# The last two expert pairs and the final LayerNorm of a transformer layer reordered across TensorE, VectorE, ScalarE and GpSimd

## Chip, cores and metric

The kernel runs on one core of one Trainium2 chip. The metric is the device time of one execution in microseconds (us); the time of the kernel before is the median of three runs.

## What is computed

One layer of a streaming encoder over 512 tokens of 1024 channels, in fp32. Only the second half of it matters here: a hierarchical mixture of experts (a group is chosen, then two experts in it), a residual, and a LayerNorm.

```python
x = _layer_norm(ALPHA * x + mixed, ln1_g, ln1_b)
ffn = _hierarchical_moe(x.reshape(b * s, d), ...)
return _layer_norm(ALPHA * x + ffn, ln2_g, ln2_b)

# one expert of 4 groups x 8, D_EXPERT = 256
hid = silu(x @ w_gate[g, e]) * (x @ w_up[g, e])
y = y + combine[:, g, e] * (hid @ w_down[g, e])
```

## The kernel before

Both attentions, the gates and the output projection fill most of the time before 418 us, where the experts begin. TensorE then runs through the 32 experts in the loop at L1332 to L1365. Each expert e has 64 slots for tokens; two experts make a pair p = e // 2, so that the gathered rows of a pair (xg, fetched by index from DRAM) are one tile of 128 x 1024. An expert's weights are six tiles of 512 KB in fp32, streamed in a fixed sequence on SP's queue (`raw_load`, L1052) and taken in the same sequence (`weights`).

The steps of an expert are these. `prep_x(p)` transposes a pair's rows on TensorE (L1108) and copies them out of PSUM, one half on ScalarE (L1086), one on VectorE (L1088). `gate_up(e)` multiplies them with four weight tiles: 16 matmuls into the PSUM tile sc, in two halves of the partitions, which ScalarE (L1134) and VectorE (L1135) add up to gus. `act(e)` transposes gus on TensorE (stp, L1142) and makes the hidden rows sg: silu on ScalarE (L1144), the product on VectorE (L1148). `down(e)` is 8 matmuls into the PSUM tile tr; ScalarE and VectorE weight the result, add the residual (L1196, L1198, L1200), and GpSimd scatters a pair's rows to the DRAM buffer y2D (`store`). The down product stands one expert late in the loop.

The last two pairs (NLATE = 2: experts 28 to 31) are called late. Their results do not go through DRAM: `down` makes their sums on VectorE (L1181), rounds them to the high part on ScalarE (L1186), and takes the low part on VectorE (L1188), both into the tile late. It needs the other half of the partitions too, for which `late_x(p)` copies xg to xo on ScalarE (L1159, L1160). A one-hot matrix stl then brings each row to its token: `fin_add` multiplies it with late into PSUM banks called fin (fin<-late,stl), two banks for each of the four token tiles of 128. The other experts' rows come back from y2D as two tiles yy per token tile (L1233, behind the last weights on SP's queue); they are added to each other on GpSimd (L1272, Y_POOL) and go into the same banks by an identity matmul (`fin_rows`, fin<-yy,ident).

`finish` works off the list FIN, which is written by hand: a word is a step, its number the expert, the tile or bank.tile. "add2.3" adds late experts to bank 2 until three are in it, "rows0" adds tile 0's row pair, "stat0.1" and "stat1.1" are the statistics of tile 1's two banks on VectorE (L1294, L1296), "root0" to "root3" the steps of the reciprocal root (`rstd_parts`: aggregation on VectorE L778, Ln and Exp on ScalarE L782 and L783, a Newton step of three operations on VectorE L786, L788, L790), "gain" the product with the LayerNorm gain on VectorE (L1312), "end" the scale by the root and the bias: for tile 3 on VectorE (L1320), for the others on ScalarE (L1328) and GpSimd (L1329). FIN_AT says behind which gate_up the first four banks are opened; late results that exist by then are added there.

TensorE's instructions run in program order wherever `in_order` is set (`pin`, `keep_in_program_order`), and so do those of the other engines that are pinned. What is not pinned is placed by a scheduler, which also sets the order of the gain rows (`gain_rows`: copies bc on VectorE, matmuls pj<-ident,bc, copies gb on ScalarE) among the work of experts 28 and 29.

Of the kernel before, what the change touches and what calls it, by code (L numbers as in the profile page):

```python
# [18 lines left out]
P = 128  # L19
# [60 lines left out]
NLATE = 2  # L80
Y_PE = ()
Y_POOL = (0, 1, 2, 3)
F_DVE = (3,)
G_ACT = ()
FIN_TAG = ("pj", "pj", "tr", "sc", "sc", "av", "tr", "tr")
FIN_AT = {30: (0, 1, 2, 3)}
FIN = (
# [16 lines left out]
def trunk(ctx, tc, xT, x, wm, wv, wbr, wout, wr, br, bg, rbx, lnp, lncol, wexp, out):  # L104
# [669 lines left out]
    def rstd_parts(pool, bs, bufs=2, between=None, eps=(epsc, EPS)):  # L774
# [16 lines left out]
        yield r, mean  # L791

    def rstd(*a, **b):
        *_, out = rstd_parts(*a, **b)
        return out
# [326 lines left out]
    def gate_up(e):  # L1122
        ps = pb.tile([P, 512], F32, tag="sc", name="sc", bufs=2)
        for c in range(C):
            if c % 2 == 0:
                w = weights()
            if e < 4:
                st = xe[0, c // 4][:, c % 4, e * CAP : (e + 1) * CAP]
            else:
                st = xp[e // 2][:, c, e % 2 * CAP : (e % 2 + 1) * CAP]  # L1130
            side = slice(c % 2 * CAP, c % 2 * CAP + CAP)
            mm(ps[side], st, w[:, c % 2 * 512 : c % 2 * 512 + 512], c < 2, c >= C - 2)
        gus[e] = bp.tile([CAP, 512], F32, tag="gus", name="gus", bufs=GUSB)
        nc.scalar.activation(gus[e], ps[CAP:], AF.Copy)  # L1134
        nc.vector.tensor_add(gus[e], gus[e], ps[:CAP])  # L1135

    hid = {}

    def act(e):
        st = pb.tile([P, 4, CAP], F32, tag="av", name="stp", bufs=1)  # L1140
        for q in range(4):
            pin(nc.tensor.transpose(st[:, q, :], gus[e][:, q * P : (q + 1) * P], ident[:CAP, :CAP]))  # L1142
        sg = bp.tile([P, 2, CAP], F32, tag="sg", name="sg", bufs=3)
        nc.scalar.activation(sg, st[:, 0:2, :], AF.Silu)  # L1144
        if e == NE - 1:
            load = nc.scalar.preload_act_table_set("natural_log_exp_and_others")
            tc.keep_in_program_order(load)
        nc.vector.tensor_mul(sg, sg, st[:, 2:4, :])  # L1148
        hid[e] = sg
# [5 lines left out]
    def late_x(p):  # L1155

        xo[p] = slot([P, D], F32, f"xo{p}", slots2)
        a, b = slice(0, CAP), slice(CAP, P)
        nc.scalar.activation(xo[p][b, S:], xg[p][a, S:], AF.Copy)  # L1159
        nc.scalar.activation(xo[p][a, :S], xg[p][b, :S], AF.Copy)  # L1160

    def down(e):
        p, odd = e // 2, e % 2
        is_late = p >= NPAIR - NLATE
        if is_late:
            late.append(hip.tile([P, D], F32R, tag="hi", name=f"late{e}"))
# [8 lines left out]
        if is_late:  # L1175
# [11 lines left out]
            for half, here in enumerate(sides):  # L1187
                pin(nc.vector.tensor_sub(  # L1188
                    late[-1][sides[1 - half], cs[half]], sums[here, cs[half]], late[-1][here, cs[half]].bitcast(F32)
# [84 lines left out]
    def finish():  # L1274

        for step in FIN:
# [20 lines left out]
            elif what == "root0":  # L1297
                parts[tt] = rstd_parts(bp, fs[tt], TT, None, (epsf, 4.0 * EPS / ALPHA**2))
                fr[tt] = next(parts[tt])
# [33 lines left out]
    for e in range(NE):  # L1333
# [16 lines left out]
        if e % 2 and 3 <= e < NE - 1:  # L1350
            prep_x(e // 2 + 1)
        act(e)
        in_order[0] = False
        if e == 4:
# [6 lines left out]
        if e == NE - 4:  # L1361
            gain_rows()
            last_rows()
        if e % 2 == 0 and e >= NE - 2 * NLATE:
            late_x(e // 2)  # L1365
    in_order[0] = True
# [117 lines left out]
```

## Time and profile before

| | |
|---|---|
| runs | 689.62, 691.15, 689.78 us |
| median | 689.78 us |
| profiled execution | 692.57 us, its span 690.8 us |
| busy: TensorE (PE) | 643.6 us, 93% of the span |
| busy: VectorE (DVE) | 417.3 us, 60% |
| busy: ScalarE (ACT) | 319.0 us, 46% |
| busy: GpSimd (POOL) | 108.2 us, 16% |
| mean granted clock of TensorE | 0.98 of full speed |

The profile is of one execution, and its rows add up to that execution's span. A timeline row is a group of equal instructions that follow each other on one engine: its start, its length, and, in brackets, how long the engine had been idle and what ended that. PEclk is the granted clock of TensorE as a share of 2.4 GHz. A share of busy time is a mean over stages with different limits, so the stages are read one by one.

### The profile page before, as it was taken

Reading aid. Unit: us, or ns where it says so; the run is one execution under the profiler, and the core shown is the slowest. Engines: PE = TensorE matmul, PEld = TensorE weight load, DVE = VectorE, ACT = ScalarE, POOL = GpSimd, SP = SyncE. Lnnn points to the kernel's source line nnn. Section 1 sums busy time; section 2 is a strip of 40 time slices with the busy share of each in tenths; the row PEclk is TensorE's granted clock in tenths of the full one; section 3 lists DMA queues with packets and bytes.
Section 4 is the critical chain, followed back from the end, with each engine's and each line's share of the span. In section 5 each row is a group of like instructions: output and inputs, shape, how many; then the busy total and the mean of one; then the engine's idle time right before and its main releaser. Section 6 shows DMA issues by size and latency. Waiting matters only on the chain.

```text
span 690.8 us, 8912 instructions
## 1 busy us (share of the span) xinstructions
PE 643.6 (93%) x3108; PEld 420.8 (61%) x3108; DVE 417.3 (60%) x850; ACT 319.0 (46%) x626; POOL 108.2 (16%) x152
## 2 busy tenths in 40 slices
PE   8999999999999999989999987999999988899782
PEld 4888788887878888878888774333434322234241
DVE  5675868678867886563935994234444333334487
ACT  5676877866755565545513223322333222223422
POOL 2012112102010110050000341112112111110233
PEclk9999999999999999999999999999999999999887
DMA  8600069202130322128774579999999999999803
GB/s 331 248 0 1 1 225 353 63 0 93 46 106 17 123 77 92 46 88 304 263 315 163 202 274 412 405 411 410 409 409 405 408 406 407 402 400 405 338 3 124
DMA packets 48032, 158.62 MB, mean 230 GB/s; under 512 B 7529, under 2 KB 7673, under 8 KB 47984
## 3 DMA queue, kind: packets, MB, share of 16 engines
q1 hardware_dynamic: 43632, 150.16, 57.2%
q0 software_dynamic: 4352, 7.85, 3.0%
q8 instruction: 26, 0.43, 0.3%
q14 instruction: 22, 0.18, 0.1%
HBM read 150.16 MB, written 15.73 MB: 240 GB/s over the span
## 4 chain that ended last, share of the span: by engine, by line
PE 60%; DVE 15%; DMA 14%; ACT 6%; issue 3%; POOL 0%; SPq 0%; DVEq 0%; POOLq 0%; ACTq 0%
PE pj L130 18%; PE sc L130 13%; DMA we<-in_wexp_dram 13%; PE pb L130 6%; PE tr L130 6%; PE po L130 4%; PE pv L130 2%; PE av L130 2%; DVE t L482 2%; DVE wl L115 2%; PE tr L536 2%; DMA raw<-in_wm_dram 1%; PE stp L1142 1%; PE pj L1108 1%; ACT wh L112 1%
## 5 line engine op out<-in xcount | busy, mean ns | idle before, releaser
L130 PE MATMUL sc<-we,xp 128*64 128x512 f32 x448 | 109.8, 613 | 7.5 <-DMA we<-in_wexp_dram 6.1
L130 PE MATMUL pj<-xh,wh 128*128 128x512 f32 x256 | 103.7, 405 | 1.1 <-ACT wh L112 1.0
L130 PE MATMUL pj<-xl,wh 128*128 128x512 f32 x256 | 100.8, 394 | 0.0
L130 PE MATMUL pj<-xh,wl 128*128 128x512 f32 x256 | 100.6, 393 | 0.0
L115 DVE TENSOR_TENSOR wl<-raw,wh 128x1024 fp32r<-128x1024 f32 (+1 forms) x57 | 69.9, 1230 | 23.1 <-ACT wh L112 22.9
L1135 DVE TENSOR_TENSOR gus<-gus,sc 64x512 f32<-64x512 f32 x32 | 21.7, 679 | 94.3 <-ACT gus L1134 94.3
L130 PE MATMUL tr<-we,sg 128*64 128x512 f32 x256 | 66.0, 626 | 3.2 <-DMA we<-in_wexp_dram 2.5
L112 ACT ACTIVATE wh<-raw 128x1024 fp32r<-128x1024 f32 (+1 forms) x57 | 58.7, 1037 | 19.0 <-DMA raw<-in_wbr_dram 4.8
L130 PEld LDWEIGHTS sc<-we,xp 128*64 128x64 f32 x448 | 27.9, 138 | 64.5 <-issue 33.2
L1134 ACT ACTIVATE gus<-sc 64x512 f32<-64x512 f32 x32 | 19.0, 594 | 101.6 <-PE sc L130 101.6
L130 PEld LDWEIGHTS pj<-xh,wh 128*128 128x128 f32 x256 | 48.4, 189 | 10.9 <-ACT wh L112 1.9
L130 PEld LDWEIGHTS pj<-xh,wl 128*128 128x128 f32 x256 | 48.3, 189 | 10.8 <-DVE wl L115 0.2
L130 PEld LDWEIGHTS pj<-xl,wh 128*128 128x128 f32 x256 | 48.5, 190 | 8.2
L130 PEld LDWEIGHTS tr<-we,sg 128*64 128x64 f32 x256 | 17.3, 141 | 44.0 <-issue 34.0
L130 PE MATMUL pb<-y,wh 128*128 128x512 f32 x128 | 40.1, 394 | 0.3 <-DVE k L345 0.3
L115 DVE TENSOR_TENSOR wl<-tr,wh 128x512 fp32r<-128x512 f32 (+1 forms) x64 | 30.9, 484 | 11.9 <-ACT wh L112 11.6
L1207 POOL DMA_INDIRECT y2D<-oe,rowi x14 | 14.0, 1000 | 145.3 <-DVE oe L1198 144.7
L489 POOL TENSOR_SCALAR_AFFINE_SELECT w<-w 128x128 f32<-128x128 f32 x32 | 16.1, 515 | 126.0 <-ACT w L486 115.2
L112 ACT ACTIVATE wh<-tr 128x512 fp32r<-128x512 f32 (+1 forms) x64 | 27.3, 428 | 12.5 <-PE tr L536 12.2
L130 PE MATMUL sc<-k,q 128*128 128x512 f32 (+3 forms) x128 | 28.5, 323 | 0.2
L536 PE MATMUL tr<-ident,w 128*128 128x128 f32 x160 | 27.8, 272 | 0.0
L1200 DVE SCALAR_TENSOR_TENSOR oe<-tr,wslot,xg 64x512 f32<-64x512 f32 x24 | 18.0, 750 | 16.3 <-PE tr L130 15.8
(227 smaller groups left out, 1218.5 us busy)
## 6 DMA issues: line engine op xcount, KB each, us to landing
we<-in_wexp_dram SPq DMA_DIRECT2D x192, 512.0 KB
raw<-in_wm_dram SPq DMA_DIRECT2D x32, 512.0 KB
raw<-in_wv_dram SPq DMA_DIRECT2D x8, 512.0 KB
y2D<-zero SPq DMA_DIRECT2D x16, 256.0 KB
raw<-in_wbr_dram SPq DMA_DIRECT2D x8, 512.0 KB
raw<-in_wout_dram SPq DMA_DIRECT2D x8, 512.0 KB
yy<-y2D SPq DMA_DIRECT2D x8, 512.0 KB
strip<-in_rbx_dram SPq DMA_DIRECT2D x8, 256.0 KB
```

Of the source, the lines that this page charges most:

```text
L112: act = nc.scalar.activation(hi, src, AF.Copy)
L115: pin((eng or nc.vector).tensor_sub(lo, src, hi.bitcast(F32)), fix == "both")
L130: pin(nc.tensor.matmul(ps, a, b, start=start, stop=stop))
L482: nc.vector.tensor_tensor_scan(out=t[:, ::-1], data0=t[:, ::-1], data1=mk[:, ::-1], initial=0.0, op0=OP.add, op1=OP.mult)
L489: nc.gpsimd.affine_select(out=blk, in_=blk, pattern=[[-1, P]], compare_op=OP.is_gt, fill=0.0, base=0, channel_multiplier=1)
L536: nc.tensor.transpose(tr[:, i * P : (i + 1) * P], w[:, off + j * P : off + (j + 1) * P], ident)
L1108: pin(nc.tensor.transpose(ps[:, c, :], xg[p][:, o : o + P], ident))
L1134: nc.scalar.activation(gus[e], ps[CAP:], AF.Copy)
L1135: nc.vector.tensor_add(gus[e], gus[e], ps[:CAP])
L1142: pin(nc.tensor.transpose(st[:, q, :], gus[e][:, q * P : (q + 1) * P], ident[:CAP, :CAP]))
L1200: nc.vector.scalar_tensor_tensor(out=dst, in0=ps[here], scalar=wslot[here, p : p + 1], in1=xg[p][here, cs], op0=OP.mult, op1=OP.add)
L1207: nc.gpsimd.indirect_dma_start(out=y2D[:, :], out_offset=bass.IndirectOffsetOnAxis(ap=rowi[:, p : p + 1], axis=0), in_=oe[p], in_offset=No ...
```

## The change

The order of the last steps is written anew. The first four fin banks are opened behind gate_up(31) instead of gate_up(30). down(31) follows down(30) at once, and the adds of experts 29, 30 and 31 come behind both. The row pairs of tiles 0 and 1 are no longer added on GpSimd: each of their two yy tiles goes through its own identity matmuls. Of the low parts of the last pair (experts 30 and 31), the second half moves from VectorE to GpSimd. The final LayerNorm's Newton step is computed by four small ScalarE operations (`rstd_act`). The operations that make gus, sg and xo are pinned to program order, and late_x stands behind an odd expert's act.

```diff
--- before.py
+++ after.py
@@ -78,15 +78,15 @@
 WHB = 3
 DEPTH = 2
 NLATE = 2
-Y_PE = ()
-Y_POOL = (0, 1, 2, 3)
+Y_PE = (0, 1)
+Y_POOL = (2, 3)
 F_DVE = (3,)
 G_ACT = ()
 FIN_TAG = ("pj", "pj", "tr", "sc", "sc", "av", "tr", "tr")
-FIN_AT = {30: (0, 1, 2, 3)}
+FIN_AT = {31: (0, 1, 2, 3)}
 FIN = (
-    "sum0 sum1 sum2 sum3 down30 add0.2 add1.2 add2.2 add3.2 down31 add0.3 add1.3 add2.3 add3.3 rows0 add0.4 add1.4 stat0.0 "
-    "stat1.0 rows1 add2.4 add3.4 root0.0 gain0.0 root1.0 gain1.0 root2.0 root3.0 end.0 open4 add4.4 open5 add5.4 rows2 "
+    "down30 down31 add0.2 add1.2 add2.2 add3.2 rows0 sum2 sum3 add0.3 add1.3 add0.4 add1.4 stat0.0 "
+    "stat1.0 add2.3 add3.3 rows1 add2.4 add3.4 root0.0 gain0.0 root1.0 gain1.0 root2.0 root3.0 end.0 open4 add4.4 open5 add5.4 rows2 "
     "open6 add6.4 open7 add7.4 rows3 stat0.1 stat1.1 root0.1 gain0.1 root1.1 gain1.1 root2.1 root3.1 stat0.2 stat1.2 end.1 "
     "root0.2 gain0.2 root1.2 gain1.2 root2.2 root3.2 stat0.3 stat1.3 end.2 root0.3 "
     "gain0.3 root1.3 gain1.3 root2.3 root3.3 end.3"
@@ -790,6 +790,23 @@
         pin(nc.vector.tensor_mul(r, r, u))
         yield r, mean
 
+    def rstd_act(pool, bs, bufs, eps):
+
+        mv = pool.tile([P, 5], F32, tag="mv", name="mv", bufs=bufs)
+        mean, var, r, u, ve = (mv[:, k : k + 1] for k in range(5))
+        pin(nc.vector.bn_aggr(mv[:, 0:2], bs))
+        pin(nc.vector.tensor_scalar(out=ve, in0=var, scalar1=eps[1], scalar2=None, op0=OP.add))
+        pin(nc.scalar.activation(r, var, AF.Ln, bias=eps[0]))
+        pin(nc.scalar.activation(r, r, AF.Exp, scale=-0.5))
+        yield r, mean
+        pin(nc.scalar.activation(u, r, AF.Square))
+        pin(nc.scalar.activation(u, u, AF.Copy, scale=ve))
+        pin(nc.scalar.activation(u, u, AF.Copy, scale=-0.5, bias=1.5))
+        yield r, mean
+        pin(nc.scalar.activation(r, r, AF.Copy, scale=u))
+        yield r, mean
+        yield r, mean
+
     def rstd(*a, **b):
         *_, out = rstd_parts(*a, **b)
         return out
@@ -1131,8 +1148,8 @@
             side = slice(c % 2 * CAP, c % 2 * CAP + CAP)
             mm(ps[side], st, w[:, c % 2 * 512 : c % 2 * 512 + 512], c < 2, c >= C - 2)
         gus[e] = bp.tile([CAP, 512], F32, tag="gus", name="gus", bufs=GUSB)
-        nc.scalar.activation(gus[e], ps[CAP:], AF.Copy)
-        nc.vector.tensor_add(gus[e], gus[e], ps[:CAP])
+        pin(nc.scalar.activation(gus[e], ps[CAP:], AF.Copy))
+        pin(nc.vector.tensor_add(gus[e], gus[e], ps[:CAP]))
 
     hid = {}
 
@@ -1141,11 +1158,11 @@
         for q in range(4):
             pin(nc.tensor.transpose(st[:, q, :], gus[e][:, q * P : (q + 1) * P], ident[:CAP, :CAP]))
         sg = bp.tile([P, 2, CAP], F32, tag="sg", name="sg", bufs=3)
-        nc.scalar.activation(sg, st[:, 0:2, :], AF.Silu)
+        pin(nc.scalar.activation(sg, st[:, 0:2, :], AF.Silu))
         if e == NE - 1:
             load = nc.scalar.preload_act_table_set("natural_log_exp_and_others")
             tc.keep_in_program_order(load)
-        nc.vector.tensor_mul(sg, sg, st[:, 2:4, :])
+        pin(nc.vector.tensor_mul(sg, sg, st[:, 2:4, :]))
         hid[e] = sg
 
     oe = {}
@@ -1156,12 +1173,13 @@
 
         xo[p] = slot([P, D], F32, f"xo{p}", slots2)
         a, b = slice(0, CAP), slice(CAP, P)
-        nc.scalar.activation(xo[p][b, S:], xg[p][a, S:], AF.Copy)
-        nc.scalar.activation(xo[p][a, :S], xg[p][b, :S], AF.Copy)
+        pin(nc.scalar.activation(xo[p][b, S:], xg[p][a, S:], AF.Copy))
+        pin(nc.scalar.activation(xo[p][a, :S], xg[p][b, :S], AF.Copy))
 
     def down(e):
         p, odd = e // 2, e % 2
         is_late = p >= NPAIR - NLATE
+        odd_last = p == NPAIR - 1
         if is_late:
             late.append(hip.tile([P, D], F32R, tag="hi", name=f"late{e}"))
         elif not odd:
@@ -1185,7 +1203,7 @@
             for half, here in enumerate(sides):
                 pin(nc.scalar.activation(late[-1][here, cs[half]], sums[here, cs[half]], AF.Copy))
             for half, here in enumerate(sides):
-                pin(nc.vector.tensor_sub(
+                pin((nc.gpsimd if half and odd_last else nc.vector).tensor_sub(
                     late[-1][sides[1 - half], cs[half]], sums[here, cs[half]], late[-1][here, cs[half]].bitcast(F32)
                 ))
             return
@@ -1295,7 +1313,7 @@
             elif what == "stat1":
                 pin(nc.vector.bn_stats(fs[tt][:, 1, :], fin[2 * tt + 1]))
             elif what == "root0":
-                parts[tt] = rstd_parts(bp, fs[tt], TT, None, (epsf, 4.0 * EPS / ALPHA**2))
+                parts[tt] = rstd_act(bp, fs[tt], TT, (epsf, 4.0 * EPS / ALPHA**2))
                 fr[tt] = next(parts[tt])
             elif what.startswith("gain"):
                 k = int(what[4:])
@@ -1350,6 +1368,8 @@
         if e % 2 and 3 <= e < NE - 1:
             prep_x(e // 2 + 1)
         act(e)
+        if e % 2 and NE - 2 * NLATE <= e + 1 < NE:
+            late_x(e // 2 + 1)
         in_order[0] = False
         if e == 4:
             for p in range(2):
@@ -1361,8 +1381,6 @@
         if e == NE - 4:
             gain_rows()
             last_rows()
-        if e % 2 == 0 and e >= NE - 2 * NLATE:
-            late_x(e // 2)
     in_order[0] = True
     finish()
     in_order[0] = False
```

The pinned order moves instructions that the diff does not show. TensorE, experts 28 and 29, before (sc is gate_up(29), tr down(28), stp the transposes of 28, pj the gain rows):

```order
L1142 MATMUL stp<-ident,gus 128x64 x4
L130 MATMUL pj<-ident,bc 128x128 x4
L130 MATMUL sc<-we_5196,xp_5480 64x512 x2
L130 MATMUL sc<-we_5200,xp_5480 64x512 x2
L130 MATMUL sc<-we_5209,xp_5480 64x512 x2
L130 MATMUL sc<-we_5213,xp_5480 64x512 x2
L130 MATMUL tr<-we_5242,sg 64x512 x2
L130 MATMUL tr<-we_5246,sg 64x512 x2
```

and now:

```order
L130 MATMUL pj<-ident,bc 128x128 x4
L130 MATMUL sc<-we_5196,xp_5480 64x512 x2
L130 MATMUL sc<-we_5200,xp_5480 64x512 x2
L130 MATMUL sc<-we_5209,xp_5480 64x512 x2
L130 MATMUL sc<-we_5213,xp_5480 64x512 x2
L1159 MATMUL stp<-ident,gus 128x64 x4
L130 MATMUL tr<-we_5242,sg 64x512 x2
L130 MATMUL tr<-we_5246,sg 64x512 x2
```

The transposes of expert 28 have moved behind gate_up(29), directly in front of the down product that reads their result.

TensorE from gate_up(30)'s end, before; of each group of equal instructions the first stands here (late_5633 and late_5710 are experts 28 and 29, late_5736 is 30; tr<-we_5309 is down(29), we_5342 and we_5346 down(30), we_5350 and we_5354 down(31); yy_5605 below is a row tile of token tile 0):

```order
L130 MATMUL fin_5679<-late_5633,stl_5592 128x512
L1142 MATMUL stp<-ident,gus 128x64 x4
L130 MATMUL sc<-we_5288,xp_5646 64x512 x2
L130 MATMUL tr<-we_5309,sg 64x512 x2
L1142 MATMUL stp<-ident,gus 128x64 x4
L130 MATMUL tr<-we_5342,sg 64x512 x2
L130 MATMUL tr<-we_5346,sg 64x512 x2
L130 MATMUL fin_5679<-late_5710,stl_5592 128x512
L130 MATMUL tr<-we_5350,sg 64x512 x2
L130 MATMUL tr<-we_5354,sg 64x512 x2
L130 MATMUL fin_5679<-late_5736,stl_5597 128x512
```

and now, where late_5732 is expert 30:

```order
L1159 MATMUL stp<-ident,gus 128x64 x4
L130 MATMUL sc<-we_5288,xp_5646 64x512 x2
L130 MATMUL fin_5702<-late_5633,stl_5595 128x512
L130 MATMUL tr<-we_5309,sg 64x512 x2
L1159 MATMUL stp<-ident,gus 128x64 x4
L130 MATMUL tr<-we_5342,sg 64x512 x2
L130 MATMUL tr<-we_5346,sg 64x512 x2
L130 MATMUL tr<-we_5350,sg 64x512 x2
L130 MATMUL tr<-we_5354,sg 64x512 x2
L130 MATMUL fin_5702<-late_5710,stl_5595 128x512
L130 MATMUL fin_5702<-yy_5605,ident 128x512
L130 MATMUL fin_5702<-late_5732,stl_5600 128x512
```

The adds of expert 28 have moved behind gate_up(31) (its first row is sc<-we_5288), those of 29 behind both down products, and the two rows of yy_5605 and its partner stand ahead of the adds of expert 30.

VectorE at the first token tile of the tail, before:

```order
L1294 BN_STATS bsf<-fin_5679 128x6
L1296 BN_STATS bsf<-fin_5680 128x6
L778 BN_AGGR mv<-bsf 128x2
L784 TENSOR_SCALAR mv<-mv 128x1
L1312 SCALAR_TENSOR_TENSOR res_5774<-fin_5679,mv,gb_5532 128x512
L786 SCALAR_TENSOR_TENSOR mv<-mv 128x1
L1312 SCALAR_TENSOR_TENSOR res_5774<-fin_5680,mv,gb_5532 128x512
L788 TENSOR_SCALAR mv<-mv 128x1
L790 TENSOR_TENSOR mv<-mv 128x1
```

and now:

```order
L1312 BN_STATS bsf<-fin_5702 128x6
L1314 BN_STATS bsf<-fin_5703 128x6
L797 BN_AGGR mv<-bsf 128x2
L798 TENSOR_SCALAR mv<-mv 128x1
L1330 SCALAR_TENSOR_TENSOR res_5772<-fin_5702,mv,gb_5535 128x512
L1330 SCALAR_TENSOR_TENSOR res_5772<-fin_5703,mv,gb_5535 128x512
L1312 BN_STATS bsf<-fin_5704 128x6
```

The three Newton operations (L786, L788, L790) have left VectorE; the next tile's statistics follow the second gain directly.

## Rows read from the trace of the kernel before

**Rows 1.** Stretches: span; busy us (count) of PE, PEld, DVE, ACT, POOL; PEclk; DMA; GB/s

```profile
409.90:413.40 3.50, 3.50 (x19) 3.50 (x19) 3.41 (x16) 0.42 (x2) 1.86 (x6) 0.51 1.01 300
421.00:425.00 4.00, 2.57 (x16) 0.92 (x14) 0.97 (x2) 2.15 (x3) 0.00 (x0) 1.00 1.02 412
600.00:640.00 40.00, 35.94 (x172) 13.27 (x168) 15.45 (x40) 10.60 (x20) 3.03 (x3) 1.00 1.02 403
642.00:648.80 6.80, 6.72 (x18) 2.86 (x20) 0.94 (x2) 1.44 (x3) 0.00 (x0) 0.50 1.02 395
```

**Rows 2.** Timeline of TensorE: start, us, instructions, [idle before, and its releaser]

```profile
409.25 0.38 PE L130 MATMUL trf<-onehot,hh 128*128 128x256 f32 x1 [1.60 <-DVE onehot L912]
...
423.59 0.46 PE L1142 MATMUL stp<-ident,gus 64*128 64x64 f32 x4 [1.43 <-DVE gus L1135]
...
631.53 1.89 PE L130 MATMUL tr<-we,sg 128*64 128x512 f32 x8
...
634.76 3.65 PE L130 MATMUL sc<-we,xp 128*64 128x512 f32 x16
642.08 2.33 PE L130 MATMUL fin<-late,stl 128*128 128x512 f32 x4 [3.67 <-DVE late L1188]
...
644.96 5.56 PE L130 MATMUL sc<-we,xp 128*64 128x512 f32 x16
```

**Rows 3.** Timeline of VectorE, from gate_up(30) to the end

```profile
639.09 0.68 DVE L1135 TENSOR_TENSOR gus<-gus,sc 64x512 f32<-64x512 f32 x1 [3.62 <-ACT gus L1134]
639.69 0.74 DVE L1181 SCALAR_TENSOR_TENSOR sum<-tr,wslot,xg 64x512 f32<-64x512 f32 x1
...
641.25 1.40 DVE L1188 TENSOR_TENSOR late<-sum,late 64x512 fp32r<-64x512 f32 x2
645.38 0.29 DVE L1148 TENSOR_TENSOR sg<-sg,stp 128x128 f32<-128x128 f32 x1 [2.73 <-ACT sg L1144]
...
655.32 4.19 DVE L1188 TENSOR_TENSOR late<-sum,late 64x512 fp32r<-64x512 f32 x2
...
669.07 0.68 DVE L1296 BATCH_NORM_STATS2 bsf<-fin 128x6 f32<-128x512 f32 x1
...
670.77 0.21 DVE L786 SCALAR_TENSOR_TENSOR mv<-mv 128x1 f32<-128x1 f32 x1
...
671.81 0.69 DVE L1294 BATCH_NORM_STATS2 bsf<-fin 128x6 f32<-128x512 f32 x1
...
674.11 1.15 DVE L786 SCALAR_TENSOR_TENSOR mv<-mv 128x1 f32<-128x1 f32 x1
...
680.34 0.69 DVE L1294 BATCH_NORM_STATS2 bsf<-fin 128x6 f32<-128x512 f32 x1
...
684.71 1.42 DVE L1320 SCALAR_TENSOR_TENSOR res<-res,mv,gb 128x512 f32<-128x512 f32 x2
```

**Rows 4.** Timeline of ScalarE, from gate_up(30) to the end

```profile
638.46 0.59 ACT L1134 ACTIVATE gus<-sc 64x512 f32<-64x512 f32 x1 [3.32 <-PE sc L130]
...
645.07 0.28 ACT L1144 ACTIVATE sg<-stp 128x128 f32<-128x128 f32 x1 [1.89 <-PE stp L1142]
...
670.03 0.29 ACT L782 ACTIVATE mv<-mv,epsf 128x1 f32<-128x1 f32 x1 [2.97 <-DVE mv L778]
670.35 0.20 ACT L783 ACTIVATE mv<-mv 128x1 f32<-128x1 f32 x1
671.93 1.33 ACT L1328 ACTIVATE res<-res,mv 128x512 f32<-128x512 f32 x2 [1.38 <-DVE mv L790]
```

**Rows 5.** Timeline of GpSimd, from 640 to the end

```profile
653.85 7.88 POOL L1272 TENSOR_TENSOR yy<-yy,yy 128x1024 f32<-128x1024 f32 x3 [0.20 <-DMA yy<-y2D]
672.73 2.52 POOL L1329 TENSOR_TENSOR res<-res,gb 128x512 f32<-128x512 f32 x2 [11.00 <-ACT res L1328]
```

**Rows 6.** Timelines of VectorE and of TensorE at an even expert

```profile
590.46 0.69 DVE L1198 TENSOR_TENSOR oe<-oe,xg 64x512 f32<-64x512 f32 x1 [0.43 <-ACT oe L1196]
...
594.27 2.26 PE L130 MATMUL tr<-we,sg 128*64 128x512 f32 x8 [0.28 <-DMA we<-in_wexp_dram]
```

## The prediction

> **What bounds the kernel now.** I read the table of stretches first. For 40 us before 640 the DMA engines are full, at 403 GB/s, and TensorE, at full clock, is busy 35.94 of 40 us [rows 1]: the expert weights set the pace, and a saving there is worth nothing. So I looked for the place where that cover ends. The weights' issues ahead of it are untouched, so the question is what happens between 638 and the end.
>
> TensorE's timeline gives the answer [rows 2]. At 642.08 it had waited 3.67 us for VectorE's low parts (L1188) of expert 28, because the one-hot adds of that expert stand in front of the last transposes and of gate_up(31). In the stretch behind it the clock is 0.50, that is 1.2 GHz of 2.4 [rows 1], and gate_up(31) takes 5.56 us where gate_up(30) took 3.65 [rows 2]. The same happens to expert 29 further on: its adds, in front of down(31), wait for two low parts that cost VectorE 4.19 us, where the pair costs 1.40 at 641.25 [rows 3]. The difference is GpSimd, which from 653.85 adds row pairs back to back [rows 5]: a VectorE subtraction with both inputs in SBUF stands still meanwhile.
>
> Then comes a tail in which VectorE alone counts: from the second statistics of tile 0 (669.07) to the end of the last output operation (684.71 + 1.42 = 686.13) it is 17.06 us [rows 3]. In it the first Newton operation takes 0.21 us for tile 0 but 1.15 for tile 1, when GpSimd adds that overlap it [rows 3, 5].
>
> **The change, part by part.**
>
> *Pinned order, up to expert 30.* The transposes of expert 28 now stand directly in front of its down product, so their latency is exposed: 0.46 on TensorE [rows 2], 0.28 on ScalarE [rows 4], 0.29 on VectorE [rows 3], together 1.0. Nothing else fills TensorE there. I count it in full: gate_up(30) ends at 634.76 + 3.65 + 1.0 = 639.4 instead of 638.4. The bounds are 0 (weights are late anyway) and 1.3. On ScalarE's queue, gus(28) now stands behind the four gain rows and the two copies of late_x(14), about 0.6 each, as a gus copy of that size [rows 4]; its reader comes only behind gate_up(29), 3.65 long, so they are hidden, and cost 1.3 if that cover were gone. SP's queue keeps its order.
>
> *Late adds behind, and down products together.* From 639.4: gus on ScalarE 0.59 [rows 4] and VectorE 0.68 [rows 3], to 640.7. Sums of expert 28, which VectorE did behind this gus, now come before it and are covered by gate_up(30). Then transposes 0.4 and gate_up(31) 3.65 to 644.7; four adds of expert 28 at half of 2.33/4, the price at half clock, 1.17, to 645.8; down(29) 1.89 to 647.7; transposes 0.4, down(30) 1.89, to 649.9 [rows 2]. down(31) needs the hidden rows of 31, and VectorE has first to do two sums of 29 at 0.75 (649.1), wait for ScalarE's rounding copy, as long as a gus copy, 0.6 (649.8), and finish the second low part, 0.70 (650.5), then sg 0.29 [rows 3, 4]: 650.8. So TensorE idles 0.9 there and down(31) ends at 652.7. Both long waits are gone, since nothing stands behind the low parts but the final adds.
>
> *Low parts on two engines.* VectorE does the sums of 30 (652.3), the first low part of 30 (653.0), the sums of 31 (654.5). ScalarE copies, 0.63 (655.1), and GpSimd takes the last low part. No row shows this 64x512 subtraction on GpSimd. Its 128x512 addition takes 2.52/2 = 1.26 [rows 5]; the ends are 0.63, half of it, if partitions count, and 1.26 if only the row's length does. I take 1.26, since VectorE's times follow the row's length too (0.70 for 64x512, 0.68 for the 128x512 statistics). That gives 656.4; one matmul and its latency, 0.5, put tile 0's second statistics at 656.95. On VectorE the same subtraction would have ended at about 656.6 behind the other one, so this edit is worth 0.2 at most. The Trainium skill, in "GPSIMD Engine Reference", section 3.1, has an elementwise add at 1.96 times VectorE's time and keeps VectorE as the rule; an estimate from it is 0.70 x 1.96 = 1.37, and the sum would be 0.1 longer. Before, those statistics began at 669.07: **12.1 us** come from here.
>
> *Row pairs of tiles 0 and 1 on TensorE.* Four more identity matmuls, some 0.4 to 0.6 each, lie between down(31)'s end and the last low parts, where TensorE has 655.2 - 652.7 less the adds of 29 (1.2): about covered; if not, it costs 1.2. Now two GpSimd sums of 7.88/3 = 2.63 [rows 5] remain, from 656.4 to 661.7; tile 2's statistics come at 662.5, tile 3's at 665.6. They no longer run beside the low parts of 29 and 30. The loads of the rows themselves are not moved.
>
> *Newton on ScalarE.* VectorE keeps two small operations. Tile 0 to tile 1 took 671.81 - 669.07 = 2.74 [rows 3]; without the three Newton operations (0.21 the first, overlapping the gain; with the two short ones I estimate 0.26 net) it is 2.48. A full period is this plus the first statistics, 0.62: 3.1. Tiles 1 and 2, 680.34 - 671.81 = 8.53 for both, become 6.2, since what GpSimd stalled is no longer on VectorE. The last, 684.71 - 680.34 = 4.37, becomes 3.4: I leave 0.3 for the wait on ScalarE's root, or on GpSimd's last add, which now ends close to VectorE's last operation. With 1.42 at the end: 2.48 + 6.2 + 3.4 + 1.42 = 13.5 instead of 17.06, **3.6 us**. ScalarE's load per tile is six small operations between 0.20 (Exp) and 0.32 (from Ln's start to Exp's) and 1.33 for the result [rows 4]: 2.5 to 3.25, against VectorE's 3.1.
>
> **Sum.** 12.1 + 3.6 = 15.7. The profiled execution took 692.57 us, its span 690.8; it becomes 676.9. It lies 2.8 above the median of the three runs, 689.78, so the same gain makes **674.1**. With the bounds above (expert 28 +-1, GpSimd's operation -0.6, matmuls +1.2, tail +-0.6) the forecast's own range is 672.6 to 675.8.
>
> **The rivals.**
>
> *The clock falls again.* TensorE still idles 1.3 us at 639.4 and 0.9 at 649.9. After 1.60 us of waiting at 409.25 the clock was 0.51; after 1.43 at 423.59 it stayed at 1.00 [rows 1, 2]. The new waits are shorter than both, which speaks against it, but more small ones stand close together. The price: the half-clock stretch behind 642.0 lasted 6.8 us, in which gate_up(31) lost 5.56 - 3.65 = 1.9, and the adds and down(29) behind it a further 0.4: 2.3, so 676.4. If down(31) loses its 1.9 as well, 678.2. Chance 0.24.
>
> *ScalarE becomes the bound of the tail.* If each small operation costs 0.35 with its wait, a tile takes 6 x 0.35 + 1.33 = 3.4 there, 0.3 over VectorE's period; three tiles and a later last root make 1.3: 675.4. For it speaks that the six depend on each other; against it that Exp takes 0.20 [rows 4]. The Trainium skill, in "ScalarE: Activation LUTs", section "Rules for kernel authors", tells authors to put additions and multiplications on VectorE, not ScalarE; by that rule this part would lose. On VectorE, though, the row is 1.15, not 0.21, whenever GpSimd adds [rows 3]. Chance 0.08.
>
> *Slower: the even experts.* Pinning puts the gated product of every even expert behind the previous expert's output rows on VectorE. Before, sg stood ahead of an addition of 0.69 that had waited 0.43 for ScalarE, at 590.46 [rows 6]; behind it, it comes 0.43 + 0.69 + 0.3 = 1.4 later, at 591.4. Its reader, the down product at 594.27, waits for a weight DMA [rows 6], so 2.9 us of slack hide it. It decides only where the delay exceeds this slack; then some 12 experts would lose more than 1.3 us each, 16 in all, and the time would be 690 or above. For it speaks only the number of experts. Chance 0.02.
>
> *The late chain was not what set the end.* If the row pairs' loads, still landing one behind the other when GpSimd starts at 653.85 (0.20 of waiting, [rows 5]), hold tile 0 up to 661, about 4 us of the 12.1 are gone: 678. The loads' order speaks against it. Chance 0.03.
>
> **Numbers.** Forecast 0.63, clock 0.24, ScalarE 0.08, loads 0.03, even experts 0.02. The prediction is the forecast's 674.1. The range goes from its lower bound, 672.5, to both falls of the clock, 678.3. About 0.2%, 1.4 us, is what a measurement of this kernel can tell from no change. All cases but the last end far below 688.4: faster 0.96, same 0.02, slower 0.02.
>
> **What would show it.** Right: no wait of TensorE over 1.5 us between 638 and 653; gate_up(31) at about 3.65; down(30) and down(31) a little over 1 us apart; tile 0's second statistics at about 657; statistics of the tiles 3.1 us apart, no VectorE operation over 0.8 us among them but the last two. A clock below 1.00 between 640 and 653 shows the first rival; VectorE waiting for ScalarE between tiles the second; waits for hidden rows instead of weights at even experts the third. I am wrong if statistics still begin after 660 at full clock, or if the stretch before 638 is longer by more than 1.3.

## The result and the profile after

Four runs of the changed kernel took 680.44 to 682.24 us, median 681.15, against 690.46 for the kernel before measured beside them: a ratio of 0.9866, 95% interval 0.9845 to 0.9887. Six more runs later had a median of 680.89, against 691.47 (0.9837, 0.9801 to 0.9872). The kernel is faster, by 9.3 us in the first set and 10.6 in the second, and not by the 15.7 that were forecast; 681.15 lies above the range.

The profiled execution took 682.24 us, its span 680.4. Executions differ by some us ahead of the first expert, whatever the kernel (its matmuls start at 418.5 and 425.1 in two profiles of the kernel before, at 420.1 and 424.4 in two of the changed one), so I compare tails from a common mark: the moment at which SP issues the first row-pair load. The experts' weights ahead of it were to take the same time in both kernels, and do within half a microsecond. TensorE's timeline at the first expert and SP's at the mark, before:

```profile
418.50 3.65 PE L130 MATMUL sc<-we,xe 128*64 128x512 f32 x16
...
639.74 9.18 SPq L1233 DMA_DIRECT2D yy<-y2D  x8
```

and after:

```profile
420.08 3.65 PE L130 MATMUL sc<-we,xe 128*64 128x512 f32 x16
...
640.83 9.17 SPq L1251 DMA_DIRECT2D yy<-y2D  x8
```

That is 221.2 us before and 220.7 after; over all profiles of this case it is 219.9 to 221.2, and 1.4 apart in the two profiles of the kernel before. From the mark to the last instruction it is 51.0 before and 39.6 after: the tail is **11.4 us** shorter, where 15.7 was forecast, 35.3. All ends below are counted from this mark.

TensorE's timeline after, with the waits in brackets:

```profile
633.65 1.94 PE L130 MATMUL tr<-we,sg 128*64 128x512 f32 x8 [0.69 <-DVE sg L1165]
...
642.00 0.46 PE L1159 MATMUL stp<-ident,gus 64*128 64x64 f32 x4 [1.41 <-DVE gus L1152]
642.38 3.65 PE L130 MATMUL sc<-we,xp 128*64 128x512 f32 x16
645.97 1.19 PE L130 MATMUL fin<-late,stl 128*128 128x512 f32 x4
...
652.42 1.94 PE L130 MATMUL tr<-we,sg 128*64 128x512 f32 x8 [1.14 <-DVE sg L1165]
...
655.32 3.60 PE L130 MATMUL fin<-yy,ident 128*128 128x512 f32 x8
...
660.13 3.60 PE L130 MATMUL fin<-yy,ident 128*128 128x512 f32 x8
663.17 2.88 PE L130 MATMUL fin<-late,stl 128*128 128x512 f32 x10
```

The waits of 3.67 us and its like [rows 2] are gone. What is left are 0.69 for expert 28's transposes, 1.41 for gus(30) and 1.14 ahead of down(31). gate_up(31) takes 3.65 us, where it took 5.56 [rows 2], and the stretches say why (span; busy us and count of PE, PEld, DVE, ACT, POOL; PEclk; DMA share; GB/s):

```profile
642.00:652.40 10.40, 9.29 (x44) 3.34 (x44) 4.16 (x8) 3.21 (x6) 0.00 (x0) 1.00 1.01 400
654.40:671.30 16.90, 16.90 (x52) 9.62 (x52) 11.96 (x23) 9.32 (x27) 12.34 (x9) 1.00 0.13 49
```

The clock stayed at 1.00, where it had been 0.50 behind the long wait [rows 1]. The second row holds the surprise: for 16.9 us TensorE is busy without a pause. The chain that ended last runs through it (start, us, what):

```profile
652.08 0.30 DVE sg L1165
652.38 0.04 issue
652.42 1.94 PE tr L130 x8
654.36 16.98 PE fin L130 x52
671.34 0.02 issue
671.36 0.71 DVE bsf L1314
```

From the end of down(31) to the last statistics, nothing but TensorE's adds into the fin banks is on the chain (52 entries of the trace, which are 40 matmuls: an fp32 matmul leaves two entries, a one-hot matmul one). VectorE, which I had as the tail's bound, waits for them:

```profile
635.64 0.74 DVE L1199 SCALAR_TENSOR_TENSOR sum<-tr,wslot,xg 64x512 f32<-64x512 f32 x1 [1.03 <-PE tr L130]
...
637.93 1.40 DVE L1206 TENSOR_TENSOR late<-sum,late 64x512 fp32r<-64x512 f32 x2
...
641.26 0.68 DVE L1152 TENSOR_TENSOR gus<-gus,sc 64x512 f32<-64x512 f32 x1 [1.61 <-ACT gus L1151]
...
659.64 0.70 DVE L1312 BATCH_NORM_STATS2 bsf<-fin 128x6 f32<-128x512 f32 x1 [2.83 <-PE fin L130]
660.25 0.68 DVE L1314 BATCH_NORM_STATS2 bsf<-fin 128x6 f32<-128x512 f32 x1
...
664.00 0.70 DVE L1312 BATCH_NORM_STATS2 bsf<-fin 128x6 f32<-128x512 f32 x1 [1.30 <-PE fin L130]
...
666.96 0.69 DVE L1312 BATCH_NORM_STATS2 bsf<-fin 128x6 f32<-128x512 f32 x1
...
670.51 0.70 DVE L1312 BATCH_NORM_STATS2 bsf<-fin 128x6 f32<-128x512 f32 x1 [0.27 <-PE fin L130]
...
674.03 1.42 DVE L1338 SCALAR_TENSOR_TENSOR res<-res,mv,gb 128x512 f32<-128x512 f32 x2 [0.20 <-ACT mv L806]
```

The first three rows show the reordering that helped: expert 28's sums and low parts now stand ahead of gus(30), so they are done at 639.3; before, they began behind it [rows 3]. The rest shows the tail: first statistics of the tiles at 659.64, 664.00, 666.96 and 670.51, that is periods of 4.36, 2.96 and 3.55, not 3.1. GpSimd's new operations, and ScalarE's four of the Newton step at tile 0:

```profile
654.61 1.28 POOL L1206 TENSOR_TENSOR late<-sum,late 64x512 fp32r<-64x512 f32 x1 [23.47 <-ACT late L1204]
656.83 1.26 POOL L1206 TENSOR_TENSOR late<-sum,late 64x512 fp32r<-64x512 f32 x1 [0.94 <-ACT late L1204]
```

```profile
661.77 0.20 ACT L802 ACTIVATE mv<-mv 128x1 f32<-128x1 f32 x1
662.00 0.29 ACT L803 ACTIVATE mv<-mv 128x1 f32<-128x1 f32 x1
662.33 0.20 ACT L804 ACTIVATE mv<-mv 128x1 f32<-128x1 f32 x1
662.57 0.30 ACT L806 ACTIVATE mv<-mv 128x1 f32<-128x1 f32 x1
```

### The profile page after: what moved, and what is told of

It is laid out like the page before. It is cut to its first block, busy times and chain, and to the rows that moved or that the text cites. A ratio compares the mean times of both kernels' runs of the same rounds, so it can differ in the third digit from the quotient of the medians.

```text
span 680.4 us, 8940 instructions
## 1 busy us (share of the span) xinstructions
PE 640.9 (94%) x3116; PEld 420.4 (62%) x3116; DVE 408.2 (60%) x836; ACT 322.6 (47%) x642; POOL 105.1 (15%) x152
## 4 chain that ended last, share of the span: by engine, by line
PE 52%; DMA 20%; DVE 15%; ACT 7%; issue 3%; POOL 0%; SPq 0%; DVEq 0%; POOLq 0%; ACTq 0%
DMA we<-in_wexp_dram 18%; PE pj L130 16%; PE sc L130 10%; PE pb L130 7%; PE po L130 4%; PE tr L130 4%; DVE t L482 3%; PE fin L130 2%; PE pv L130 2%; DVE wl L115 2%; PE av L130 2%; ACT wh L112 2%; DVE t L480 1%; PE tr L536 1%; DMA raw<-in_wm_dram 1%
## 5 line engine op out<-in xcount | busy, mean ns | idle before, releaser
L130 PE MATMUL sc<-we,xp 128*64 128x512 f32 x448 | 108.1, 604 | 7.4 <-DMA we<-in_wexp_dram 5.6
L115 DVE TENSOR_TENSOR wl<-raw,wh 128x1024 fp32r<-128x1024 f32 (+1 forms) x57 | 69.9, 1230 | 23.0 <-ACT wh L112 22.8
L130 PE MATMUL tr<-we,sg 128*64 128x512 f32 x256 | 63.3, 601 | 5.3 <-DMA we<-in_wexp_dram 2.6
L130 PEld LDWEIGHTS tr<-we,sg 128*64 128x64 f32 x256 | 16.4, 136 | 44.9 <-issue 31.5
L1214 ACT ACTIVATE oe<-tr,wswap 64x512 f32<-64x512 f32 x28 | 19.1, 682 | 26.0 <-DVE oe L1218 25.7
```

What stands on the lines that cost most here:

```text
L115: pin((eng or nc.vector).tensor_sub(lo, src, hi.bitcast(F32)), fix == "both")
L130: pin(nc.tensor.matmul(ps, a, b, start=start, stop=stop))
L1214: nc.scalar.activation(dst, ps[here], AF.Copy, scale=(wslot if half == odd else wswap)[here, p : p + 1])
```

## The experiments

All times in us; "end" and the first statistics of tiles 0 and 3 are counted from the mark, from each kernel's profile. Ratios are against the kernel before, timed beside it; its median there was 690.46 to 691.72, so a ratio is not the quotient of two medians of this table.

| kernel | stat. tile 0 | stat. tile 3 | end | median | ratio, 95% interval |
|---|---|---|---|---|---|
| before | 28.7 | 40.6 | 51.0 | 690.46 | |
| e11 before, again | 28.4 | 40.3 | 50.7 | 697.53, one run | |
| changed | 18.8 | 29.7 | 39.6 | 681.15 | 0.9866, 0.9845 to 0.9887 |
| e14 changed, again | 18.8 | 29.6 | 39.4 | 680.89 | 0.9837, 0.9801 to 0.9872 |
| e1 half the pairs | 17.2 | 26.8 | 36.6 | 679.15 | 0.9852, 0.9797 to 0.9908 |
| e2 Newton on VectorE | 18.9 | 31.5 | 42.0 | 683.48 | 0.9893, 0.9847 to 0.9938 |
| e3 low parts on VectorE | 19.5 | 30.7 | 40.5 | 682.54 | 0.9872, 0.9836 to 0.9909 |
| e4 no pins | 22.6 | 33.7 | 43.7 | 686.29 | 0.9937, 0.9904 to 0.9970 |
| e5 early adds | 17.6 | 28.4 | 38.2 | 678.74 | 0.9825, 0.9808 to 0.9842 |
| e6 one pair on TensorE | 19.0 | 28.7 | 38.4 | 678.66 | 0.9835, 0.9815 to 0.9856 |
| e8 three moves more | 16.3 | 26.7 | 36.4 | 677.64 | 0.9801, 0.9784 to 0.9819 |
| e9 old tail | 22.8 | 31.8 | 41.9 | 682.20 | 0.9881, 0.9860 to 0.9902 |
| e10 pins alone | 22.8 | 34.7 | 45.4 | 686.94 | 0.9885, 0.9827 to 0.9943 |
| e12 sum on VectorE | 16.3 | 25.5 | 35.4 | 676.23 | 0.9756, 0.9706 to 0.9807 |
| e13 Newton alone | 28.6 | 37.5 | 47.7 | 687.74 | 0.9933, 0.9893 to 0.9972 |

**e1, half of the row pairs left out.** This kernel leaves out the second row tile of tiles 0 and 1, so half of these rows' contribution is missing from its result; it only puts a price on the four added matmuls. My theory after the result: TensorE's added identity matmuls are on the path.

```diff
-for n, t in enumerate(y2[tt] if tt in Y_PE else y2[tt][:1]):
-    fin_rows(tt, t, n == 1 or tt not in Y_PE)
+for t in y2[tt][:1]:
+    fin_rows(tt, t, True)
```

> The changed kernel without the second row tile of token tiles 0 and 1: the four added identity matmuls are gone, and with them half of these rows' contribution. Theory (in the changed kernel TensorE has no pause from the end of down(31) to the last statistics, so what I took as covered is on the path, at about 0.9 us a matmul): 2.4 to 3.4 us below the changed kernel's 681.2, so 677.8 to 678.8, and VectorE's waits for TensorE between tiles gone. Rival (VectorE's and GpSimd's low parts still set the start of the tail and VectorE its length, so the matmuls are covered, as predicted): 0 to 1 us below, 680.2 to 681.2.

The end came at 36.6, 3.0 earlier, as the theory has it; the median, 679.15, is 2.0 lower and so just above the 677.8 to 678.8 that I expected. TensorE's and VectorE's timelines:

```profile
654.61 1.88 PE L130 MATMUL fin<-yy,ident 128*128 128x512 f32 x4
```

```profile
657.22 0.70 DVE L1312 BATCH_NORM_STATS2 bsf<-fin 128x6 f32<-128x512 f32 x1 [1.14 <-PE fin L130]
...
660.39 0.70 DVE L1312 BATCH_NORM_STATS2 bsf<-fin 128x6 f32<-128x512 f32 x1
```

Two identity matmuls fewer per tile are 3.60 - 1.88 = 1.72 us: 0.86 each. VectorE's first period is now 3.2, close to the 3.1 of the sum. It is not free of TensorE everywhere: 0.27 and 0.16 of waits remain at tile 3.

**e2, Newton on VectorE again.**

```diff
-parts[tt] = rstd_act(bp, fs[tt], TT, (epsf, 4.0 * EPS / ALPHA**2))
+parts[tt] = rstd_parts(bp, fs[tt], TT, None, (epsf, 4.0 * EPS / ALPHA**2))
```

> The changed kernel with the Newton step on VectorE as before. Theory (TensorE is the tail's bound, so Newton on ScalarE bought little): 0.5 to 1.8 us above 681.2, that is 681.7 to 683.0. Rival (Newton on ScalarE is worth what the prediction gave it): 3 to 3.6 us above, 684.2 to 684.8.

The end is 2.4 later, between the two. VectorE's first Newton operation is held up by GpSimd again. VectorE's and GpSimd's timelines at tile 2:

```profile
669.18 1.15 DVE L786 SCALAR_TENSOR_TENSOR mv<-mv 128x1 f32<-128x1 f32 x1
```

```profile
667.81 2.50 POOL L1347 TENSOR_TENSOR res<-res,gb 128x512 f32<-128x512 f32 x2 [1.77 <-ACT res L1346]
```

At tile 0 to 1 TensorE's period of 4.36 hides all of it; at the later tiles VectorE's 4.0 to 4.3 count, where TensorE left 3.0 and 3.6.

**e3, all low parts on VectorE.**

```diff
-pin((nc.gpsimd if half and odd_last else nc.vector).tensor_sub(
+pin(nc.vector.tensor_sub(
```

> The changed kernel with all low parts of experts 30 and 31 on VectorE. Theory: TensorE reaches the late adds of tile 0 at 658.4 in the profile, the low part on GpSimd is ready at 658.1; on VectorE the last low part is ready at 658.2 to 658.4, so within 0.4 us of 681.2. Rival (sharing frees VectorE by 1.4 us in the chain that sets the end): 1 to 1.4 us above, 682.2 to 682.6.

The end is 0.9 later, the median 1.4: about the rival's size, but not for its reason. VectorE's and GpSimd's timelines show what neither had:

```profile
660.45 3.52 DVE L1206 TENSOR_TENSOR late<-sum,late 64x512 fp32r<-64x512 f32 x2
```

```profile
661.06 2.36 POOL L1290 TENSOR_TENSOR yy<-yy,yy 128x1024 f32<-128x1024 f32 x1 [26.33 <-DMA yy<-y2D]
```

Without low parts in front of them, GpSimd's sums start as soon as their rows land, in the middle of VectorE's last pair, which takes 3.52 instead of 1.40. Without this stall the pair would have ended at 661.85, 17.3 from the mark, and GpSimd's last low part in the changed kernel ends there too (658.09, 17.3). So what the share is worth is that it keeps GpSimd's own sums back.

**e4, without the pins.**

```diff
-pin(nc.scalar.activation(gus[e], ps[CAP:], AF.Copy))
-pin(nc.vector.tensor_add(gus[e], gus[e], ps[:CAP]))
+nc.scalar.activation(gus[e], ps[CAP:], AF.Copy)
+nc.vector.tensor_add(gus[e], gus[e], ps[:CAP])
...
-        if e % 2 and NE - 2 * NLATE <= e + 1 < NE:
-            late_x(e // 2 + 1)
+        if e % 2 == 0 and e >= NE - 2 * NLATE:
+            late_x(e // 2)
```

sg and xo are unpinned in the same way.

> The changed kernel with gus, sg and xo placed by the scheduler again and late_x where it was. Theory (the pinned order exposes expert 28's transposes, 1.0 us, and nothing else): 0.5 to 1.2 us below 681.2, so 680.0 to 680.7, with down(28) ahead of where it is now. Rival 1 (the pinned order also delays the even experts, which would show as a loss before 600 us): 2 us or more below. Rival 2 (without the pins the late sums of expert 28 slide behind gus(30) again, and the adds behind gate_up(31) come to wait): 0 to 2 us above.

It is 4.1 worse at the end, 5.1 in the median, more than any theory had, in the direction of the second rival. gate_up(31) starts 1.07 earlier from the mark, so the 1.0 that the prediction charged for expert 28 is right; but VectorE now makes the sums of expert 28 at 645.4, behind even gus(31), and TensorE waits for the low parts:

```profile
647.67 0.50 PE L130 MATMUL fin<-late,stl 128*128 128x512 f32 x1 [3.58 <-DVE late L1206]
...
649.46 3.40 PE L130 MATMUL tr<-we,sg 128*64 128x512 f32 x8
```

```profile
649.00:652.40 3.40, 3.40 (x10) 0.76 (x8) 0.00 (x0) 0.00 (x0) 0.00 (x0) 0.50 1.02 406
```

Behind a wait of 3.58 the clock is at 0.50 again, and down(29) takes 3.40.

**e9, e10 and e13: the parts in the old tail.** e9 has the pins (and late_x moved with them) and Newton on ScalarE, with the old list, opening, row pairs and low parts; e10 has the pins and the moved late_x alone, e13 Newton alone. The diff shows e9's main lines, against the changed kernel.

```diff
-FIN_AT = {31: (0, 1, 2, 3)}
+FIN_AT = {30: (0, 1, 2, 3)}
-Y_PE = (0, 1)
-Y_POOL = (2, 3)
+Y_PE = ()
+Y_POOL = (0, 1, 2, 3)
```

with FIN as before and all low parts on VectorE.

> The kernel before with the pinned order and the Newton step on ScalarE alone: list of steps, opening of the banks, row pairs on GpSimd and low parts on VectorE are the old ones. Theory (the pins bring expert 28's low parts ahead of gus(30), and so take away the first long wait of TensorE and the low clock behind it; the low parts of 29 still collide with GpSimd's sums): the end comes 51.0 - 4 to 6 = 45 to 47 us from the first row-pair load's issue; gate_up(31) at full clock. Rival (the new list is what takes the waits away; pins alone change nothing): 48.5 or more, that is, Newton's share of 2.4 only.

> The kernel before with the pinned order and late_x moved, nothing else. The pinned order and Newton on ScalarE together bring the end from 51.0 to 41.9 us behind the first row-pair load's issue. Theory (the pins take away the first long wait and the low clock behind it, Newton is worth some 2.4 to 3.6 by itself): 44.3 to 45.5. Rival (the two parts need each other, since the tail's stalls on VectorE hide what the pins gain): 47 or more.

> The kernel before with the Newton step on ScalarE, nothing else. Theory (in the old tail GpSimd's sums and result adds stall VectorE's Newton operation in three of four tiles, and TensorE, done with tile 3 by 678, is not the limit there): 2.8 to 3.6 us off the end, 47.4 to 48.2 behind the first row-pair load's issue. Rival (the last tiles' matmuls take VectorE's place at once): 1.5 to 2.4 off, 48.6 to 49.5.

Ends: 41.9, 45.4, 47.7, against 51.0. So the pins alone are worth 5.6, Newton alone 3.3, and both 9.1: they add up. Pins and Newton do better than the 45 to 47 I expected for e9. The new list, the row pairs on TensorE and the shared low parts bring the remaining 2.3 of 11.4. This is their worth behind the other two, and not their worth alone: without the pins (e4) the list, the row pairs, the low parts and Newton together gain 51.0 - 43.7 = 7.3, and Newton alone 3.3, so some 4 is left by subtraction. By these numbers the pins and the rest overlap by some 1.5; why, was not tested. What the rest takes away is visible in e9, where VectorE still meets GpSimd's sums, TensorE waits, and the clock behind that wait is 0.50:

```profile
650.15 5.42 DVE L1206 TENSOR_TENSOR late<-sum,late 64x512 fp32r<-64x512 f32 x2
```

```profile
655.62 1.65 PE L130 MATMUL fin<-late,stl 128*128 128x512 f32 x3 [2.25 <-DVE late L1206]
```

```profile
652.46 8.10 POOL L1290 TENSOR_TENSOR yy<-yy,yy 128x1024 f32<-128x1024 f32 x3 [0.19 <-DMA yy<-y2D]
```

```profile
655.20:658.50 3.30, 2.88 (x5) 1.83 (x6) 3.17 (x5) 1.26 (x2) 3.30 (x2) 0.50 0.03 14
```

**e11 and e14, both kernels again.** e11 is the kernel before, e14 the changed one, unaltered.

> The kernel before once more, for a second profile. Theory: the two long waits of TensorE behind 638 and the half clock behind each are there in every execution, so the end comes 50.5 to 51.5 us behind the first row-pair load's issue, and what differs between executions lies before 440 us. Rival: the half clock in the tail was an accident of the first profile, and without it the end comes at 47 to 49, so that part of the expected gain was never there.

> The changed kernel once more. Theory (the tail is 11.4 us shorter in every execution, and what differs between executions lies before the first expert): its end comes 39.4 to 39.8 us behind the first row-pair load's issue again, and over more runs the median comes 10.5 to 12 below that of the kernel before, nearer to the tail's 11.4 than the first 9.3. Rival (the change costs some 2 us ahead of the tail): the median stays 9 to 10 below, and the first expert's matmuls start later than in the kernel before in the new profile too.

The tails repeat within 0.3: 50.7 and 39.4. In e11 the wait and the half clock are back:

```profile
647.39 2.34 PE L130 MATMUL fin<-late,stl 128*128 128x512 f32 x4 [3.67 <-DVE late L1188]
```

```profile
646.60:653.40 6.80, 6.01 (x16) 2.63 (x18) 1.62 (x3) 2.13 (x4) 0.00 (x0) 0.50 1.02 405
```

What differs lies ahead of the experts: in e14 the stretch from 300 to 418 has a clock of 0.93, against 0.99 before, and the first expert starts at 424.4, in a kernel whose first profile has 420.1. The kernel before does the same: e11 has 0.93 in that stretch and its first expert at 425.1, so a late start comes without the change too, which speaks against the rival. The second median, 10.6 below, is nearer to 11.4 than the first, 9.3; with intervals 3 to 5 us wide I leave the rest open.

**e5 and e6: shortening TensorE's path.** e5 puts expert 28's adds into the pause ahead of the transposes of 30; e6 has only tile 0's pair on TensorE.

```diff
-FIN_AT = {31: (0, 1, 2, 3)}
+FIN_AT = {30: (0, 1, 2, 3)}
```

```diff
-Y_PE = (0, 1)
-Y_POOL = (2, 3)
+Y_PE = (0,)
+Y_POOL = (1, 2, 3)
...
-... add3.2 rows0 sum2 sum3 ...
+... add3.2 rows0 sum1 sum2 sum3 ...
```

> The changed kernel with the adds of expert 28 back behind gate_up(30), where TensorE waits 1.41 us for gus(30). Theory (TensorE is the bound behind down(31), and expert 28's low parts are ready at 639.3, before gate_up(30) ends at 640.6): the four adds, 1.19 us, disappear in that pause, and the time from the first row-pair load's issue to the end of the span, 39.6 us in the changed kernel, falls by 1.1 to 38.5. Rival (the chain of low parts on VectorE, ScalarE and GpSimd sets the end): it falls by less than 0.4, or, if the low parts come late as in the kernel before, it grows by 1 or more.

> The changed kernel with tile 1's row pair added on GpSimd again, but behind the last low part; only tile 0's goes through TensorE. Theory: TensorE's second identity adds of tile 1, 1.7 us, leave the path; tile 1's statistics come 1.3 to 1.7 earlier, and the end 1 to 1.7 earlier (38.0 to 38.6 from the first row-pair load's issue). Rival (covered adds; GpSimd's three sums, 2.35 each, now hold tiles 1 to 3): no gain, or up to 1 later.

e5 ends at 38.2, 1.4 earlier; the adds fit into the pause:

```profile
638.64 1.20 PE L130 MATMUL fin<-late,stl 128*128 128x512 f32 x4
640.12 0.46 PE L1159 MATMUL stp<-ident,gus 64*128 64x64 f32 x4 [0.28 <-DVE gus L1152]
```

e6 ends at 38.4, 1.2 earlier: of 1.7 us saved, TensorE gives 0.3 back in a wait for GpSimd's sum, and tile 1's statistics come 1.0 earlier, not 1.3 to 1.7. Both hold for TensorE as the bound.

**e8 and e12: both paths shortened.** e8 joins e5 and e6, puts expert 31's sg between the two sums of 29, 29's second low part on GpSimd, and the table load (ScalarE's load of its function tables, 1.28 us, L1163) behind the last rounding copy. Of its edit, the lines on the hidden rows and the low part:

```diff
+                if e == NE - 3 and half:
+                    act(NE - 1)
...
-pin((nc.gpsimd if half and odd_last else nc.vector).tensor_sub(
+pin((nc.gpsimd if half and (odd_last or e == NE - 3) else nc.vector).tensor_sub(
```

> e5 and e6 together, and three more moves: expert 31's hidden rows between the two sums of 29, the second low part of 29 on GpSimd, the table load behind the last rounding copy. Theory (both paths have to be shortened, TensorE's by its pause before down(31), 1.14 us, the low parts' by 0.7 on VectorE): the last low part is ready at about 656 on the changed kernel's clock instead of 658.1, tile 0's statistics come 1.7 earlier, tile 3's 3.5 to 4 earlier, the end 35.6 to 36.3 from the first row-pair load's issue, so 677.2 to 677.9 if the rest stays. Rival (TensorE's order is not what limits): less than 1.5 us in all.

It ends at 36.4, just outside what I expected (35.6 to 36.3); tile 0's statistics come 2.5 earlier (1.7 expected), tile 3's 3.0 (3.5 to 4 expected). TensorE waited 0.96 for GpSimd's sum of tile 1:

```profile
657.85 1.99 PE L130 MATMUL fin<-yy,ident 128*128 128x512 f32 x4 [0.96 <-POOL yy L1292]
```

e12 makes that sum on VectorE (`fin_sum` adds there what stands in neither Y_PE nor Y_POOL) and moves the last low part of 31 there too. Its edit against e8, cut:

```diff
-Y_POOL = (1, 2, 3)
+Y_POOL = (2, 3)
-... down31 add0.2 add1.2 add2.2 add3.2 rows0 sum1 sum2 sum3 ...
+... down31 sum1 add0.2 add1.2 add2.2 add3.2 rows0 sum2 sum3 ...
-... if half and (odd_last or e == NE - 3) ...
+... if half and e in (NE - 3, NE - 2) ...
```

> e8_best_guess with tile 1's row pair added on VectorE and the last low part of expert 31 back on VectorE. There TensorE waited 0.96 us for GpSimd's sum of tile 1. Theory (TensorE is the bound from down(31) on): this wait goes, tile 0's statistics stay at 16.3 us behind the first row-pair load's issue or come up to 0.4 earlier, tile 1's and all behind them come 0.8 to 1.0 earlier, the end at 35.4 to 35.7. Rival (VectorE's addition of 128x1024 meets GpSimd's sums and stands still): tile 0's statistics 1 us or more later, the end at 37 or more.

It ends at 35.4, as expected. VectorE's sum, which no GpSimd operation meets, takes 1.23, and TensorE goes on without the wait:

```profile
652.95 1.23 DVE L1292 TENSOR_TENSOR yy<-yy,yy 128x1024 f32<-128x1024 f32 x1
```

```profile
653.11 1.95 PE L130 MATMUL fin<-late,stl 128*128 128x512 f32 x6
654.89 1.88 PE L130 MATMUL fin<-yy,ident 128*128 128x512 f32 x4
```

e12 is the fastest kernel here: its ratio to the kernel before is 0.9756 (0.9706 to 0.9807), its median 676.23, and its tail is 4.2 us shorter than the changed kernel's, beside which it was not timed.

## Why the prediction was wrong

The direction and the mechanism up to down(31) were right; the tail's bound and the size were not. In the tail, 35.3 was forecast and 39.6 measured, 4.3 short: 2.2 of it is there at tile 0's second statistics (19.4 from the mark, 17.2 forecast), 1.7 between them and the end of the last VectorE operation (15.2, 13.5 forecast), 0.4 behind that.

**The step that failed is "Row pairs of tiles 0 and 1 on TensorE".** I gave the four added identity matmuls "some 0.4 to 0.6 each" and called them "about covered; if not, it costs 1.2". They take 0.86 each (e1). The row that would have told me was in the trace of the kernel before, TensorE's timeline at tile 0:

```profile
666.30 1.88 PE L130 MATMUL fin<-yy,ident 128*128 128x512 f32 x4
```

These are two matmuls, shown as four entries since an fp32 matmul leaves two; I took half of the price. Even at that price four take 1.6 to 2.4, and my sum left 1.3 for them (655.2 - 652.7 - 1.2). I had also put all four ahead of the last low parts. The list has only tile 0's two there; "rows1" stands behind "stat1.0", so the other two lengthen the way from tile 0 to tile 1, which took 4.36 and not 3.1. e1 puts the four at 3.0 of the missing 4.3: 1.65 in front of tile 0's statistics, the rest at the tiles behind and at the end. With them goes the reading that in the tail "VectorE alone counts". It did before; once VectorE was relieved, TensorE's 40 adds, 16.98 us, were the longer row, and no rival of mine had TensorE as the tail's bound.

**Newton on ScalarE** was put at 3.6. In the old tail it is worth 3.3 (e13); in the new one 2.4 (e2), because TensorE's own periods, 4.36 behind tile 0 and 3.55 behind tile 2, take VectorE's place there. The small ScalarE operations take 0.20 to 0.30, so the second rival did not come true: VectorE waited 0.20 for the last root. The rule in the Trainium skill, "ScalarE: Activation LUTs", section "Rules for kernel authors", that multiplications belong on VectorE does not decide here: these are 128x1 operations, and on VectorE the first of them stood still for GpSimd, 1.15 instead of 0.21.

**The low part on GpSimd** was put at 0.2 at most; it is worth 0.9 (e3), for a reason that I had not seen: it delays GpSimd's own sums past VectorE's low parts. Its duration, 1.26 to 1.28, is what I took from the 128x512 row; the estimate by the Trainium skill's "GPSIMD Engine Reference", section 3.1, was 1.37.

**The pinned order** cost 1.0 at expert 28, as charged (e4: 1.07). I had the sums of expert 28 ahead of gus(30) in the chain, but booked that gain under the late adds. The list alone does not bring it: without the pins the tail is 4.1 longer (e4), and the pins alone give 5.6 (e10), so what I called a loss is worth 4.1 to 5.6, more than Newton or, behind the pins, the list. Which of the pinned operations or the place of late_x does it was not tested.

**Rivals.** The clock did not fall: behind waits of 1.41 and 1.14 it stayed at 1.00, and both forecast places kept full speed. The even experts did not wait: 220.7 us from the first expert to the mark, against 221.2. The loads did not hold tile 0: its row pairs went into TensorE at 655.3 without a wait.

**What remains.** e1, without the four matmuls, still ends 1.3 behind the forecast. Of this 0.7 is there at tile 0's second statistics (17.9 from the mark, 17.2 forecast), most of it already at the end of down(31) (13.6, 13.0 forecast); 0.35 lies between them and the end of the last VectorE operation, where TensorE still sets tile 3, and 0.2 behind that. These small gaps were not studied. The sum of 15.7 adds up; the ends of its range stand there twice, 0.1 apart (672.6 and 672.5, 678.2 and 678.3), which changes nothing.

## What to carry to other kernels

When a change relieves the engine that bounds a stage, add up the next engine's work in that stage before taking the relieved engine's time as the new length: here TensorE's adds were in the trace before, hidden in VectorE's stalls. Price an instruction by the group's time over the program's instructions, not over the trace's entries. And test a reordering part by part, in the old order and in the new: a few pinned instructions gave 5.6 of the 11.4 us alone and 4.1 last, and the rewritten list, with all that goes with it, 2.3 behind them.

## What the runs showed of the hardware

An fp32 identity matmul of 128x512 takes 0.86 us at full clock (e1: two fewer take 1.88 instead of 3.60), a one-hot matmul of the same size with rounded operands (fin<-late, high and low part) 0.23 (after: ten take 2.88, eight 2.42): adding rows through TensorE in fp32 costs more than three times as much.

GpSimd's subtraction of 512 columns takes as long for 64 partitions (1.26 to 1.28) as its addition for 128 (1.26, half of 2.52 [rows 5]).

A VectorE operation with two SBUF inputs that meets a GpSimd addition waits for it: 5.42 (e9) and 3.52 (e3) instead of 1.40 for a pair. The sums, which read one input from PSUM, are not held up: 0.76 in the kernel before, in the middle of GpSimd's 7.88 [rows 5]:

```profile
659.54 0.76 DVE L1181 SCALAR_TENSOR_TENSOR sum<-tr,wswap,xo 64x512 f32<-64x512 f32 x1
```

Waits of TensorE of 3.58 (e4) and 3.67 us (before, e11) were each followed by a granted clock of 0.50, that is 1.2 GHz, and so was one of 2.25 in e9; those of 1.41 and 1.14 were not. The length of one wait does not settle it: the clock also fell behind one of 1.60 [rows 1, 2].
